# Attention of a hybrid encoder step on one TensorE: both kv heads of a pair in one unit

## The chip, the cores and the metric

One core of one Trainium2 chip. The metric is the device time of one execution of the whole program in microseconds (us); for one core that is its own time. TensorE (PE) multiplies, VectorE (DVE), ScalarE (ACT) and GpSimd (POOL) do the element-wise work, and SyncE's queue issues most transfers.

## The reference, cut to what matters

The step runs two trunk layers over 1024 prompt tokens and 8 x 16 sample tokens, 1024 features wide. Layer 0 mixes with S5 and a gated delta rule, layer 1 with sliding-window attention, and each is followed by a gated feed-forward. The change lies in layer 1's attention: 16 heads of 64 features share 4 kv heads (4 heads each), a prompt chunk of 64 tokens sees the keys of its own and the two chunks before, a sample sees 128 cached keys and its own 16, and each row has a sink beside its scores.

```python
scores = jnp.einsum('bnqkgd,bnskd->bnkgqs', q, kband).astype(jnp.float32) * (SWA_HEAD_DIM ** -0.5)
scores = jnp.where(valid[None, :, None, None, None, :], scores, -1e30)
p = sink_softmax(scores, sinks).astype(vband.dtype)
o = jnp.einsum('bnkgqs,bnskd->bnqkgd', p, vband).reshape(bsz, L, SWA_HEADS * SWA_HEAD_DIM)
return o @ wo, k[:, -KV_WIN:], v[:, -KV_WIN:]
```

## The kernel before, in words

Activations lie with features on partitions and tokens on the free axis. A dense product is three float32r passes over operands split into a rounded part and a remainder: `gemm_block` (lines 301 to 311) issues 24 matmuls of 384 tokens into one PSUM bank, and `project` (lines 1502 to 1554) does the same for the output projection by halves of the features, 12 matmuls a half (lines 1514 to 1516). A plain fp32 product, as attention uses, stands in the trace as two matmuls and two weight loads.

`swa` (from line 1776) makes keys `kT` and values `vT`, then the queries of kv pair 0 (`qgemm(0)`), attends with them (`attend(0, ...)`, line 1940), makes the queries of pair 1, splits pair 0's output into operands (lines 1943 to 1946), attends with pair 1 and calls `project`. A pair is two kv heads; the first has its 64 features on the lower half of the partitions, the second on the upper half. `attend` runs 16 prompt units, one for each chunk of 64 tokens, then 8 sample units.

`prompt_unit` (lines 1852 to 1890) loops over the two heads e. For each: two score products into a `pS` bank (line 1862, 64 rows of the array, up to 192 keys); a softmax over both rows groups (`soft`, lines 1833 to 1850); up to four transposes into a `pT` bank (line 1882); one DVE copy of it into `sT` (lines 1885 and 1887); and one or two output products into the head's half of the partitions of a `pO` bank (line 1889), one for each 128-token tile that the keys touch. A chunk from number 2 on touches two tiles, one with all 128 keys and one with 64. After both heads the bank is evicted: by ACT for pair 0 (line 1940), by ACT and then DVE for pair 1 (lines 1951 and 1952). `sample_unit` (lines 1894 to 1914) has both heads in one bank: for each head a score product with 128 cached keys (line 1899) and one with 16 new keys (line 1900), then one softmax, two transposes, a copy, and for each head an output product with the cached values and one with the new ones (lines 1912 and 1913).

`soft` reduces the maximum on DVE (line 1837), makes the negative, clipped maximum (1838) and the sink's term (1839, 1840), takes the exponential of each row group on ACT with its sum (1842), adds and inverts (1843, 1844), and normalises group 0 on POOL (1850) and group 1 on ACT (1848).

Banks and buffers: two banks each for `pS`, `pT` and `pO` (line 1823), three softmax tiles (line 1824), two `sT`. The order of the instructions on each engine is not the source's: a planner (the tile context of line 1973) lists every instruction of the program with its dependences and its reuse of buffers and, for each engine, takes the earliest traced one of those that its own model of time holds ready. `Sooner` (line 260) moves evictions ahead. So dense products that are traced later, those of `qgemm(1)` and of `project`, stand between the attention's products in PE's queue wherever the planner found none of the attention ready; they are called fill below. Once planned, each engine's order is fixed.

Of the kernel before, what the change touches and what calls it, by code (L numbers as in the profile page):

```python
"""Hybrid S5 / gated-DeltaNet / sliding-window encoder step on one core.

Activations are held as [feature on partitions, token on the free axis]; the 1024 prompt tokens come
first, then the 8 x 16 sample tokens. A dense product is three float32r passes over operands split
exactly into a rounded part and its remainder."""
# [10 lines left out]
F32 = mybir.dt.float32  # L16
# [28 lines left out]
def ksplit(w):  # L45
    """[K, M] -> [M/128, 128 (k in its chunk), K/128 * 128] panels."""
    k, m = w.shape
    return np.ascontiguousarray(w.reshape(k // 128, 128, m // 128, 128).transpose(2, 1, 0, 3).reshape(m // 128, 128, k))


def halves(w):
    """[1024, 1024] -> [K halves, M/256, 128, 2 * 512] panels."""
    return np.ascontiguousarray(ksplit(w).reshape(4, 2, 128, 2, 512).transpose(3, 0, 2, 1, 4).reshape(2, 4, 128, 1024))


def cols(v):
    """[n * 128] -> [128, n]."""
    return np.ascontiguousarray(v.reshape(-1, 128).T)


def head_order():
    """Column order of q: row halves of a 128-tile hold a head of an even and of an odd kv group."""
    o = []
    for pair in range(2):
        for i in range(4):
            for par in range(2):
                h = 4 * (2 * pair + par) + i
                o += list(range(64 * h, 64 * h + 64))
    return np.array(o)


def s5_order():
    """Order of the S5 channels inside each 128: (channel of a group, group)."""
    return np.arange(512).reshape(4, 8, 16).transpose(0, 2, 1).reshape(512)


def layout(a):
    """The kernel's inputs: moved, copied and zero-padded only."""
# [52 lines left out]
def constants():  # L131
    """Depend on shapes alone."""
# [55 lines left out]
class Chunks:  # L188
    """Chunks of features in tiles of two: x[:, chunk, tokens]."""
# [4 lines left out]
    def new(self, i, shape, dt=F32):  # L194
        """A tile in the place of the i-th."""
# [7 lines left out]
def body(tc, nc, I, O):  # L203
# [19 lines left out]
    def mphase(**tags):  # L223
        """Five banks for the parts between the dense products: one ring, or one for each of the named tiles."""
# [25 lines left out]
    def behind(i, *others):  # L250
        """Queue an instruction behind others of its engine."""
# [4 lines left out]
    def log_tables(*others):  # L256
        """One load of the tables that Ln and Exp share, behind other activations."""
        return behind(S.preload_act_table_set("natural_log_exp_and_others"), *others)

    class Sooner:  # L260
        """Instructions inside go before others that are ready, as if traced n instructions earlier."""
# [16 lines left out]
    def parts(raw, pool=None, bufs=2):  # L278
        """Rounded part and remainder of a panel of weights."""
# [11 lines left out]
    def slots(name):  # L291
        """Per token block, the rounded part and the remainder of 4 + 4 chunks of features."""
# [24 lines left out]
    def sums(sq, w, tag=None):  # L317
        """Sum over partitions of sq, on all partitions (a bank)."""
# [11 lines left out]
    def square_in(x, k, b, i, new, parts, keep=None):  # L330
        """Squares of a chunk into partial sums over chunks; the partial sums with the last chunk.

        One running sum by GpSimd (and one by VectorE), and the last chunk's squares on their own."""
# [15 lines left out]
    def rms(r, b, parts, first=0):  # L349
        """1 / sqrt(mean of squares + eps) of a block's tokens, on all partitions, from parts of the sums of squares."""  # L350
# [18 lines left out]
    def norm(w, h, r, new, first, keep=None):  # L369
        """What fills the scales and, where there are, the operands of a norm as chunk k of block b of x, its i-th, is final."""  # L370
# [36 lines left out]
    # up_0 = -(0 + 10 + 3 + 14) - z - 1      up_1 = 15 - y - 2 - 5 + 6 + 7       up_2 = y + 0 + 10 + s  # L407
    # with z = 12 + 15, v = 13 + 16, y = 13 - P17 and s = 2 + 5 + P11, each number the product of that number.
# [31 lines left out]
    def reserve(pool):  # L440
        """Place for split panels at the bottom of a pool."""
# [3 lines left out]
    def ffn(x, pre, l, w, nxt):  # L445
# [3 lines left out]
        # gate and up  # L449
# [37 lines left out]
        # sums of weights, split panels, and what the products make  # L487
# [14 lines left out]
        def weights(raw, ps, place=place):  # L502
            """Rounded parts and remainders of the left operands of up to four products."""
# [22 lines left out]
        def tile_of(f, raw, room, order, panels, early=False):  # L526
            """The products of a tile of f: those without the last block of tokens, then the others."""
# [9 lines left out]
            def prods(p, *ps, more=False):  # L537
                """Products into p; more of them, added to what has been read already."""
# [126 lines left out]
        # the first two tiles of f, while the operands of the twenty are made  # L665
# [48 lines left out]
        # x comes back; until then half of its place is for more panels  # L714
# [19 lines left out]
        # down, by pairs of tiles of f; the products of two pairs go to sums of the seven over all pairs  # L734
# [17 lines left out]
        def load(f):  # L752
            """A tile of f, and room for another block."""
# [12 lines left out]
        def right(ps, last):  # L766
            """Right operands of two pairs, and places for those of the pair that is multiplied plainly."""
# [28 lines left out]
        def into(terms, m, o, first=False):  # L796
            """The products of the terms, tile m of their columns, added to o."""
# [10 lines left out]
        # the last pair is multiplied plainly, and what it gives added with products of the seven that make the same part of x  # L808
        also = {"B21": (0, 1), "T4": (4, 1), "B22": (0, 2)}
        for j in range(0, len(pairs) - 1, 2):  # L810
# [24 lines left out]
            for q in range(4):  # L835
# [5 lines left out]
                for e, n in enumerate(PANELS[q]):  # L841
                    for m in range(4):
# [6 lines left out]
                        if last:  # L849
                            # the sums of the seven make x  # L850
# [26 lines left out]
    # ------------------------------------------------------------------ layer 0  # L877
# [98 lines left out]
    # b and a rows: beta, cumulative log decay and what follows from it  # L976
# [26 lines left out]
    def gate_in(hh, zz):  # L1003
        """The gate of a head."""
# [8 lines left out]
    # S5: u, chunk operators, and the states after each chunk  # L1013
# [11 lines left out]
    # powers 1 to 16 of the step over a chunk  # L1025
# [32 lines left out]
    # prompt: scans inside 8 groups of 16 chunks, then over the groups' ends, then what each group starts with  # L1058
# [27 lines left out]
    # convolutions, and what of the delta rule needs no recurrence  # L1086
# [35 lines left out]
    def l2norms(ys, tables):  # L1122
        """Scale pairs (y, scratch, log of a factor) to unit length of every token."""
# [60 lines left out]
    # inverses of the delta rule's triangular systems' blocks: 32 tokens, one block to a partition  # L1184
# [29 lines left out]
    # S5 outputs  # L1214
# [28 lines left out]
    # v  # L1243
# [25 lines left out]
    # S5: operands of the GLU  # L1269
# [16 lines left out]
    # delta rule, recurrence over 128-token tiles  # L1286
# [13 lines left out]
    def solved(TT, kg, vt, t, uu, wt, tag):  # L1300
        """u and w of a tile from the transposed inverse of its system."""
# [18 lines left out]
    def finish(o, zs, t):  # L1320
        """Gated norm of a tile's output, into the operands of the output projection."""
# [16 lines left out]
    def solve_pair(t):  # L1338
        """Transposed inverses of the systems of tiles t and t + 1."""
# [13 lines left out]
        # the inverse's off-diagonal blocks, from 32 to 64 and from 64 to 128: -T11 B T00  # L1353
# [32 lines left out]
    # delta rule, the samples' step  # L1386
# [91 lines left out]
    # GLU, and the output projection of its half  # L1478
# [25 lines left out]
    def project(name, ap, x, opnd, view, w, between, places=()):  # L1504
        """An output projection, into x and the operands of the next norm: the first half of its features, but most of it for
# [471 lines left out]
```

## Time and profile before

| | |
|---|---|
| Median of 3 runs | 2831.71 us (2828.5 to 2837.01) |
| Span of the profiled execution | 2835.9 us; no other time is given for this execution |
| PE busy | 2618.7 us, 92% of the span |
| DVE, POOL, ACT busy | 1977.8, 1639.5, 1103.2 us |
| First to last score product of the stage | 1616.0 to 1914.2 us |
| Last eviction of the stage | 1934.1 us |

How to read it: busy time of PE counts the matmuls that the trace shows; two that overlap count once. A row of the timeline merges neighbours of one line: its first number is the start in us from the span's start, its second the length from there to the end of the last of them, and the last (x4) how many there are. The granted clock is a share of full speed, 1.00 being 2.4 GHz and 0.50 being 1.2 GHz.

### The profile page before, as it was taken

The numbers are of one execution on the slowest core, as the hardware profiler recorded it, in microseconds if no ns is written. First come the engines' busy times: TensorE is split into PE (matmuls) and PEld (weight loads), VectorE is DVE, ScalarE is ACT, GpSimd is POOL, SyncE is SP. The second block draws the span as 40 slices with busy tenths as digits, with TensorE's granted clock in tenths as the row PEclk, the third lists the DMA queues.
The fourth block names the chain that finished last, engine by engine and source line by source line (L and its number), as shares of the span: only waits on it lengthen the run. The fifth ranks groups of instructions, "written<-read, shape, count | busy, mean of one in ns | idle before, by whom it ended". The sixth has DMA issues, their size and how long they took to land.

```text
span 2835.9 us, 40158 instructions
## 1 busy us (share of the span) xinstructions
PE 2618.7 (92%) x14777; PEld 2422.3 (85%) x14777; DVE 1977.8 (70%) x3195; ACT 1103.2 (39%) x2232; POOL 1639.5 (58%) x1659
## 2 busy tenths in 40 slices
PE   7898999998799999989999999998799999989996
PEld 6787898897799899989999966668789999979996
DVE  7757855568876666698866245557877666688977
ACT  4233574443433333343333144433333333344332
POOL 8659332225687777788532012114587777788744
PEclk9999999998899999989999999898899999989998
DMA  6523376531122222243213100202022222243311
GB/s 199 155 74 98 107 248 205 180 121 66 56 94 70 70 70 70 70 161 120 91 43 108 59 16 23 89 29 97 32 92 78 75 71 71 70 144 106 110 62 67
DMA packets 164165, 267.20 MB, mean 94 GB/s; under 512 B 34189, under 2 KB 123949, under 8 KB 162929
## 3 DMA queue, kind: packets, MB, share of 16 engines
q1 hardware_dynamic: 163392, 262.28, 28.8%
q8 instruction: 116, 1.90, 0.3%
q10 hardware_dynamic: 576, 2.36, 0.2%
q14 instruction: 81, 0.66, 0.1%
HBM read 186.92 MB, written 79.51 MB: 94 GB/s over the span
## 4 chain that ended last, share of the span: by engine, by line
PE 45%; POOL 22%; DVE 17%; DMA 7%; issue 5%; ACT 3%; SPq 1%; DVEq 0%; ACTq 0%; POOLq 0%
POOL x L518 8%; POOL cm L518 5%; PE pd L436 4%; PE pd L437 4%; PE pd L438 4%; DMA raw<-in_wu_dram 3%; PE pg L307 3%; PE pg L308 3%; PE pg L309 3%; DVE wlo L523 3%; PE pO L1889 2%; DMA raw<-in_wg_dram 2%; PE pg L1514 2%; PE pS L1862 2%; PE pg L1516 2%
## 5 line engine op out<-in xcount | busy, mean ns | idle before, releaser
L518 POOL TENSOR_TENSOR x<-raw 128x256 f32<-128x256 f32 (+1 forms) x372 | 353.1, 976 | 99.0 <-DMA raw<-in_wg_dram 85.5
L436 PE MATMUL pa<-u,whi 128*128 128x384 f32 x928 | 324.8, 350 | 41.4 <-DVE bt L555 14.3
L438 PE MATMUL pa<-u,wlo 128*128 128x384 f32 x928 | 311.2, 345 | 13.7 <-DVE wlo L523 13.7
L437 PE MATMUL pa<-u,whi 128*128 128x384 f32 x928 | 319.2, 344 | 1.7 <-DVE u L469 1.5
L518 POOL TENSOR_TENSOR cm<-raw 128x256 f32<-128x256 f32 (+1 forms) x244 | 236.2, 990 | 78.4 <-DVE wlo L523 28.0
L436 PE MATMUL pd<-g,whi 128*128 128x384 f32 x708 | 240.4, 340 | 0.9 <-DVE bt L555 0.9
L437 PE MATMUL pd<-g,whi 128*128 128x384 f32 x708 | 241.1, 341 | 0.0
L438 PE MATMUL pd<-g,wlo 128*128 128x384 f32 x708 | 238.2, 338 | 0.0
L436 PEld LDWEIGHTS pa<-u,whi 128*128 128x128 f32 x928 | 180.7, 195 | 55.6 <-DVE bt L555 15.9
L523 DVE TENSOR_TENSOR wlo<-x,whi 128x1024 fp32r<-128x1024 f32 (+1 forms) x132 | 155.4, 1177 | 101.7 <-ACT whi L522 101.3
L1850 POOL TENSOR_SCALAR p<-p,rd 128x192 f32<-128x192 f32 (+3 forms) x80 | 59.1, 741 | 287.4 <-DVE rd L1844 175.5
L522 ACT CAST whi<-x 128x1024 fp32r<-128x1024 f32 (+1 forms) x132 | 115.7, 876 | 236.8 <-POOL x L518 209.6
L438 PEld LDWEIGHTS pa<-u,wlo 128*128 128x128 f32 x928 | 179.2, 194 | 17.3 <-DVE wlo L523 17.3
L284 ACT CAST whi<-raw 128x1024 fp32r<-128x1024 f32 x113 | 116.3, 1049 | 178.1 <-PE pg L308 83.0
L437 PEld LDWEIGHTS pa<-u,whi 128*128 128x128 f32 x928 | 180.5, 195 | 3.4 <-DVE u L469 2.3
L436 PE MATMUL pa<-u,x 128*128 128x384 f32 x428 | 150.6, 352 | 31.0 <-ACT x L522 26.8
L285 DVE TENSOR_TENSOR wlo<-raw,whi 128x1024 fp32r<-128x1024 f32 x113 | 162.4, 1438 | 22.3 <-ACT whi L284 22.1
L437 PE MATMUL pa<-u,x 128*128 128x384 f32 x428 | 148.9, 348 | 0.0
L307 PE MATMUL pg<-h0h,whi 128*128 128x384 f32 x384 | 136.6, 356 | 12.4 <-DVE ut L941 11.4
L438 PE MATMUL pa<-u,x 128*128 128x384 f32 x428 | 143.9, 345 | 0.0
L764 DVE TENSOR_TENSOR g<-gf,g 128x384 fp32r<-128x384 f32 x132 | 136.7, 1062 | 5.8 <-ACT g L763 5.8
L436 PEld LDWEIGHTS pd<-g,whi 128*128 128x128 f32 x708 | 133.9, 189 | 1.7 <-DVE bt L555 1.6
(727 smaller groups left out, 7946.2 us busy)
## 6 DMA issues: line engine op xcount, KB each, us to landing
gf<-d_g SPq DMA_DIRECT2D x44, 576.0 KB
raw<-in_wg_dram SPq DMA_DIRECT2D x44, 512.0 KB
raw<-in_wu_dram SPq DMA_DIRECT2D x44, 512.0 KB
raw<-in_wd_dram SPq DMA_DIRECT2D x44, 512.0 KB
raw<-in_win_dram SPq DMA_DIRECT2D x21, 512.0 KB
d_r<-x SPq DMA_DIRECT2D x24, 384.0 KB
x<-d_r SPq DMA_DIRECT2D x8, 1152.0 KB
d_aq<-AQ SPq DMA_DIRECT2D x12, 576.0 KB
```

Source lines behind the costliest of these rows:

```text
L284: S.copy(hi, raw)
L285: V.tensor_sub(lo, raw, hi)
L307: PE.matmul(p[:, :BW], hi[:, c], rh, start=(i == 0), stop=False)
L308: PE.matmul(p[:, :BW], hi[:, c], rl, start=False, stop=False)
L309: PE.matmul(p[:, :BW], lo[:, c], rh, start=False, stop=(i == len(ks) - 1))
L436: PE.matmul(p, hi[:, c], uh, start=start, stop=False, skip_group_check=more)
L437: PE.matmul(p, hi[:, c], ul, start=False, stop=False, skip_group_check=more)
L438: PE.matmul(p, lo[:, c], uh, start=False, stop=stop, skip_group_check=more)
L518: (P.tensor_add if sg > 0 else P.tensor_sub)(cm[:, 256 * j:256 * (j + n)], fa, ga)
L522: S.copy(hi[:, c], src)
L523: V.tensor_sub(lo[:, c], src, hi[:, c])
L764: eng.tensor_sub(op[1], t, op[0])
```

## The change

A prompt unit takes both heads together. All four score products are issued at the unit's start, alternating between the heads (row halves) and into a bank for each head. One softmax covers four row groups, with the per-unit scalars four wide. The transposes and the copy follow head by head, and then the output products, tile by tile and alternating between the heads (column halves of one bank). A sample unit has one score product of 144 keys for each head, since the 16 new keys are copied by POOL behind the 128 cached ones, and its output products alternate as well. `pS` has four banks, `pT` and `pO` one each; the softmax tiles are two of twice the rows; `sT` has three buffers; the offset of the scores in a softmax tile changes with the parity of the chunk.

```diff
-    env["mphase"](pS=2, pT=2, pO=2)
-    NPT = 3
-    pt_ = [wk.tile([128, 2, 320], F32, name=f"p{i}") for i in range(NPT)]
+    env["mphase"](pS=4, pT=1, pO=1)
+    NPT = 2
+    pt_ = [wk.tile([128, 4, 256], F32, name=f"p{i}") for i in range(NPT)]
...
-    def soft(pS, pt, n, na, sink, off):
+    def soft(banks, pt, n, sink, off):
         sink, minus = sink
+        na = sink.shape[-1]
         ng, su, es, rd = (small(x) for x in ("ng", "su", "es", "rd"))
-        V.tensor_reduce(ng[:, :na], pS, mybir.AxisListType.X, ALU.max)
+        g = na // len(banks)
+        for i, pS in enumerate(banks):
+            V.tensor_reduce(ng[:, g * i:g * i + g], pS, mybir.AxisListType.X, ALU.max)
...
-            S.activation(pt[:, a, off:off + n], pS[:, a, :], AF.Exp, scale=0.125, bias=ng[:, a:a + 1], accum_out=su[:, a:a + 1])
+            S.activation(pt[:, a, off:off + n], banks[a // g][:, a % g, :], AF.Exp, scale=0.125, bias=ng[:, a:a + 1], accum_out=su[:, a:a + 1])
...
-            if a:
+            if a % 2:
...
     def prompt_unit(pair, c, out):
+        k0 = max(0, 64 * (c - 2))
+        n = 64 * (c + 1) - k0
+        pSv = [mbank("pS")[:, :2 * n].rearrange("p (a k) -> p a k", a=2) for e in range(2)]
+        for a in range(2):
+            for e, hs in enumerate(halves_):
+                PE.matmul(pSv[e][:, a], qpr[pair][hs, c, 2 * a:2 * a + 2, :].rearrange("p i k -> p (i k)"), kT[hs, pair, k0:k0 + n], start=True, stop=True)
+        pt = next_pt()
+        off = k0 - 64 * (c - 2) + (64 if c % 2 else 0)
+        soft(pSv, pt, n, [t[:, 4 * pair:4 * pair + 4] for t in (snk[:, 0], snk[:, 1])], off)
...
         for e in range(2):
             pT = mbank("pT")
...
+            V.tensor_copy(sT[:, :nk].rearrange("p i a k -> p (i a k)"), pT[:, :256 * nk])
+            sTs.append(sT)
+        pO = mbank("pO")
+        for i, (t, w, lo, hi) in enumerate(ks):
+            for e, hs in enumerate(halves_):
+                kv = 2 * pair + e
+                PE.matmul(pO[hs, :256], vT[lo:hi, t, 64 * kv:64 * kv + 64], sTs[e][lo:hi, i].rearrange("p a k -> p (a k)"), start=(i == 0), stop=(i == nk - 1))
         out(c, pO[:, :256].rearrange("p (i k) -> p i k", i=4))
...
     def sample_unit(pair, b, out, ck, cvt, vn):
         pS = mbank("pS")
-        for e in range(2):
-            hs = slice(64 * e, 64 * e + 64)
-            ql = qsa[pair][hs, b].rearrange("p i k -> p (i k)")
-            PE.matmul(pS[hs, 0:128], ql, ck[hs, b, :], start=True, stop=True)
-            PE.matmul(pS[hs, 128:144], ql, kT[hs, pair, TP + LS * b:TP + LS * b + LS], start=True, stop=True)
+        for hs in halves_:
+            PE.matmul(pS[hs, 0:144], qsa[pair][hs, b].rearrange("p i k -> p (i k)"), ck[hs, b, :], start=True, stop=True)
...
-        for e in range(2):
-            hs = slice(64 * e, 64 * e + 64)
+        for hs in halves_:
             PE.matmul(pO[hs, :64], cvt[:, b, hs], sT[:, 0, 0, hs], start=True, stop=False)
+        for hs in halves_:
             PE.matmul(pO[hs, :64], vn[:, b, hs], sT[0:16, 0, 1, hs], start=False, stop=True)
...
-        ck = wk.tile([128, NS, 128], F32, name="ck", tag="ck", bufs=1)
-        Q.dma_start(ck, I["ck"][:, pair].rearrange("b p t -> p b t"))
+        ck = wk.tile([128, NS, 144], F32, name="ck", tag="ck", bufs=1)
+        Q.dma_start(ck[:, :, 0:128], I["ck"][:, pair].rearrange("b p t -> p b t"))
+        P.tensor_copy(ck[:, :, 128:144], kT[:, pair, TP:].rearrange("p (b t) -> p b t", b=NS))
```

## Rows read from the trace of the kernel before

**Rows 1.** The page: PE's busy time, and the chain that ended last, by engine.
```profile
PE 2618.7 (92%) x14777; PEld 2422.3 (85%) x14777; DVE 1977.8 (70%) x3195; ACT 1103.2 (39%) x2232; POOL 1639.5 (58%) x1659
...
PE 45%; POOL 22%; DVE 17%; DMA 7%; issue 5%; ACT 3%; SPq 1%; DVEq 0%; ACTq 0%; POOLq 0%
```
**Rows 2.** Busy time by stretch: length, engines, granted clock, DMA share, GB/s.
```profile
1616.00:1936.00 320.00, 319.30 (x1638) 223.53 (x1638) 168.28 (x565) 131.89 (x505) 65.97 (x86) 0.93 0.13 42
...
1761.00:1795.00 34.00, 33.70 (x123) 22.47 (x122) 16.25 (x65) 14.06 (x63) 6.66 (x11) 0.50 0.48 173
```
**Rows 3.** Waits, 1616 to 1936 us: waiter, releaser, us, times, longest.
```profile
PE pO L1889 <- DVE sT L1887: 0.3, 1, 0.3
...
DVE sT L1885 <- PE pT L1882: 36.0, 34, 3.0
```
**Rows 4.** The chain of waits from 1616 to 1936 us, by line.
```profile
by line: PE pO L1889 22.0%; PE pS L1862 18.0%; PE pT L1882 10.2%; PE pg L1514 7.4%; PE pg L1516 6.6%; PE pg L1515 6.3%; PE pg L308 6.2%; PE pg L309 5.9%; PE pg L307 5.9%; PE pO L1912 3.3%; PE pO L1913 3.3%; PE pT L1907 2.0%; PE pS L1899 2.0
```
**Rows 5.** The timeline: one head's transposes, their copy, the output product after it.
```profile
1661.60 0.60 PE L1882 MATMUL pT<-ident,p 128*128 128x128 f32 x4
...
1662.23 0.69 DVE L1885 COPY sT<-pT 128x512 f32<-128x512 f32 x1 [2.00 <-PE pT L1882]
...
1667.74 1.22 PE L1889 MATMUL pO<-sT,vT 64*64 64x256 f32 x4
```
**Rows 6.** The timeline, PE: scores of one head, and of two next to each other.
```profile
1627.32 0.92 PE L1862 MATMUL pS<-kT,q 64*128 64x192 f32 x4
...
1655.90 0.91 PE L1862 MATMUL pS<-kT,q 64*128 64x192 f32 x4
...
1742.80 0.93 PE L1862 MATMUL pS<-kT,q 64*128 64x192 f32 x8
...
1800.70 0.93 PE L1862 MATMUL pS<-kT,q 64*128 64x192 f32 x8
```
**Rows 7.** The timeline, PE: scores at the lower clock.
```profile
1784.04 1.65 PE L1862 MATMUL pS<-kT,q 64*128 64x192 f32 x4
...
1790.94 1.65 PE L1862 MATMUL pS<-kT,q 64*128 64x192 f32 x4
```
**Rows 8.** The timeline, ACT: the two exponentials of one head.
```profile
1650.10 0.42 ACT L1842 ACTIVATE p<-pS,ng 128x192 f32<-128x192 f32 x1 [1.61 <-DVE ng L1838]
...
1650.51 0.41 ACT L1842 ACTIVATE p<-pS,ng 128x192 f32<-128x192 f32 x1
```
**Rows 9.** The timeline, PE: output products of one head, and of two in succession.
```profile
1659.81 1.22 PE L1889 MATMUL pO<-sT,vT 128*64 128x256 f32 x4
...
1797.38 2.37 PE L1889 MATMUL pO<-sT,vT 128*64 128x256 f32 x8
```
**Rows 10.** The timeline, PE: an S5 product by column halves, and transposes.
```profile
142.85 1.25 PE L1049 MATMUL pe<-U,LB 128*64 128x144 f32 x16
...
1751.09 1.09 PE L1882 MATMUL pT<-ident,p 128*128 128x128 f32 x8
```
**Rows 11.** The timeline, PE: the four transposes of one head, issued apart.
```profile
1856.98 0.27 PE L1882 MATMUL pT<-ident,p 128*128 128x128 f32 x1
...
1858.33 0.55 PE L1882 MATMUL pT<-ident,p 128*128 128x128 f32 x3
```
**Rows 12.** The timeline, PE: sample units (scores of one head, of two; output products).
```profile
1757.36 0.43 PE L1899 MATMUL pS<-ck,q 64*64 64x128 f32 x2
...
1758.16 0.44 PE L1899 MATMUL pS<-ck,q 64*64 64x128 f32 x4
...
1758.61 0.33 PE L1912 MATMUL pO<-sT,cvt 128*64 128x64 f32 x2
...
1759.63 0.44 PE L1907 MATMUL pT<-ident,p 128*128 128x128 f32 x2
```
**Rows 13.** Groups by line, 1616 to 1936 us: busy, mean ns, idle before them.
```profile
L1850 POOL TENSOR_SCALAR p<-p,rd 128x192 f32<-128x192 f32 (+3 forms) x80 | 59.1, 741 | 287.4 <-DVE rd L1844 175.5 <-DVE es L1839 48.2 <-DVE ng L1838 19.4
...
L1952 DVE TENSOR_TENSOR o1l<-pO,o1h 128x256 fp32r<-128x256 f32 (+1 forms) x24 | 8.5, 353 | 14.9 <-ACT o1h L1951 14.9
```

More of the change, by code (lines that the diff above doesn't have):

```diff
@@ L1828, in swa, with small @@
     npt = [0]
-    def small(n, w=2):
+    def small(n, w=4):
         return wk.tile([128, w], F32, name=n, tag=n, bufs=4)
-    def soft(pS, pt, n, na, sink, off):
+    def soft(banks, pt, n, sink, off):
         sink, minus = sink
+        na = sink.shape[-1]
         ng, su, es, rd = (small(x) for x in ("ng", "su", "es", "rd"))
-        V.tensor_reduce(ng[:, :na], pS, mybir.AxisListType.X, ALU.max)
+        g = na // len(banks)
+        for i, pS in enumerate(banks):
+            V.tensor_reduce(ng[:, g * i:g * i + g], pS, mybir.AxisListType.X, ALU.max)
         V.scalar_tensor_tensor(ng[:, :na], ng[:, :na], -0.125, minus, ALU.mult, ALU.min)
@@ L1850, in soft, with next_pt @@
                 P.tensor_scalar(q, q, rd[:, a:a + 1], None, op0=ALU.mult)
+    halves_ = [slice(0, 64), slice(64, 128)]
+    def next_pt():
+        npt[0] += 1
+        return pt_[npt[0] % NPT]
     def prompt_unit(pair, c, out):
-        pO = mbank("pO")
-        for e in range(2):
-            hs = slice(64 * e, 64 * e + 64)
-            kv = 2 * pair + e
-            k0 = max(0, 64 * (c - 2))
-            n = 64 * (c + 1) - k0
-            pS = mbank("pS")
-            pSv = pS[:, :2 * n].rearrange("p (a k) -> p a k", a=2)
-            for a in range(2):
-                PE.matmul(pSv[:, a], qpr[pair][hs, c, 2 * a:2 * a + 2, :].rearrange("p i k -> p (i k)"), kT[hs, pair, k0:k0 + n], start=True, stop=True)
-            pt = pt_[npt[0] % NPT]
-            npt[0] += 1
-            off = k0 - 64 * (c - 2) + 64
-            soft(pSv, pt, n, 2, [t[:, 2 * kv:2 * kv + 2] for t in (snk[:, 0], snk[:, 1])], off)
-            t1 = c // 2
-            ks = []
-            w0 = 64 if c % 2 == 0 else 0
-            for t, w in ((t1 - 1, w0), (t1, w0 + 128)):
-                if t < 0:
-                    continue
-                lo = max(k0, 128 * t) - 128 * t
-                hi = min(64 * (c + 1), 128 * t + 128) - 128 * t
-                if hi > lo:
-                    ks.append((t, w, lo, hi))
@@ L1878, in prompt_unit @@
+        t1 = c // 2
+        ks = []
+        for t, w in ((t1 - 1, 0), (t1, 128)):
+            if t < 0:
+                continue
+            lo = max(k0, 128 * t) - 128 * t
+            hi = min(64 * (c + 1), 128 * t + 128) - 128 * t
+            if hi > lo:
+                ks.append((t, w, lo, hi))
+        nk = len(ks)
+        sTs = []
+        for e in range(2):
             pT = mbank("pT")
-            sT = wk.tile([128, 2, 2, 128], F32, name="sT", tag="sT", bufs=2)
+            sT = wk.tile([128, 2, 2, 128], F32, name="sT", tag="sT", bufs=3)
@@ L1880, in prompt_unit @@
             for i, (t, w, lo, hi) in enumerate(ks):
                 for a in range(2):
-                    PE.transpose(pT[:, (2 * i + a) * 128:(2 * i + a) * 128 + 128], pt[:, a, w:w + 128], ident)
-            nk = len(ks)
-            if nk == 2:
-                V.tensor_copy(sT.rearrange("p i a k -> p (i a k)"), pT)
-            else:
-                V.tensor_copy(sT[:, 0].rearrange("p a k -> p (a k)"), pT[:, :256])
-            for i, (t, w, lo, hi) in enumerate(ks):
-                PE.matmul(pO[hs, :256], vT[lo:hi, t, 64 * kv:64 * kv + 64], sT[lo:hi, i].rearrange("p a k -> p (a k)"), start=(i == 0), stop=(i == nk - 1))
+                    PE.transpose(pT[:, (2 * i + a) * 128:(2 * i + a) * 128 + 128], pt[:, 2 * e + a, w:w + 128], ident)
@@ L1890, in prompt_unit @@
+            V.tensor_copy(sT[:, :nk].rearrange("p i a k -> p (i a k)"), pT[:, :256 * nk])
[5 more added lines that the diff above has]
+                PE.matmul(pO[hs, :256], vT[lo:hi, t, 64 * kv:64 * kv + 64], sTs[e][lo:hi, i].rearrange("p a k -> p (a k)"), start=(i == 0), stop=(i == nk - 1))
         out(c, pO[:, :256].rearrange("p (i k) -> p i k", i=4))
-    ns = npt
@@ L1894, in sample_unit @@
     def sample_unit(pair, b, out, ck, cvt, vn):
         pS = mbank("pS")
-        for e in range(2):
-            hs = slice(64 * e, 64 * e + 64)
-            ql = qsa[pair][hs, b].rearrange("p i k -> p (i k)")
-            PE.matmul(pS[hs, 0:128], ql, ck[hs, b, :], start=True, stop=True)
-            PE.matmul(pS[hs, 128:144], ql, kT[hs, pair, TP + LS * b:TP + LS * b + LS], start=True, stop=True)
-        pt = pt_[npt[0] % NPT]
-        npt[0] += 1
-        soft(pS[:, :144][:, None, :], pt, 144, 1, [t[:, pair:pair + 1] for t in (snks[:, 0], snks[:, 1])], 64)
+        for hs in halves_:
+            PE.matmul(pS[hs, 0:144], qsa[pair][hs, b].rearrange("p i k -> p (i k)"), ck[hs, b, :], start=True, stop=True)
@@ L1904, in sample_unit @@
+        pt = next_pt()
+        soft([pS[:, :144][:, None, :]], pt, 144, [t[:, pair:pair + 1] for t in (snks[:, 0], snks[:, 1])], 0)
         pT = mbank("pT")
-        sT = wk.tile([128, 2, 2, 128], F32, name="sT", tag="sT", bufs=2)
+        sT = wk.tile([128, 2, 2, 128], F32, name="sT", tag="sT", bufs=3)
         for i in range(2):
-            PE.transpose(pT[:, i * 128:i * 128 + 128], pt[:, 0, 64 + 128 * i:192 + 128 * i], ident)
+            PE.transpose(pT[:, i * 128:i * 128 + 128], pt[:, 0, 128 * i:128 + 128 * i], ident)
@@ L1908, in sample_unit @@
         V.tensor_copy(sT[:, 0].rearrange("p a k -> p (a k)"), pT[:, :256])
         pO = mbank("pO")
-        for e in range(2):
-            hs = slice(64 * e, 64 * e + 64)
+        for hs in halves_:
             PE.matmul(pO[hs, :64], cvt[:, b, hs], sT[:, 0, 0, hs], start=True, stop=False)
+        for hs in halves_:
             PE.matmul(pO[hs, :64], vn[:, b, hs], sT[0:16, 0, 1, hs], start=False, stop=True)
```

## The prediction

> **What bounds the kernel now.** The page comes first: TensorE (PE) is busy for 92% of the span, and PE work is 45% of the chain that ended last [rows 1]. Then the stage: the changed code runs from 1616 us, the first score product, to 1936 us, the last evictions. The stretch table [rows 2] shows PE busy for 319.3 of these 320 us, VectorE (DVE) for 168, ScalarE (ACT) for 132, GpSimd (POOL) for 66. The waits agree: PE itself is held up twice, for 0.3 us each, while DVE spends 36.0 us waiting for transposes alone [rows 3]. So PE's own issue time sets this stage, and the chain by line [rows 4] divides it: 22.0% (70 us) for the prompt's output products, 18.0% (58 us) for its scores, 10.2% (33 us) for its transposes, 3.3% twice for the samples' output products (21 us). The rest is mostly dense products that the planner puts between, the "fill".
>
> Two further readings decide how a faster PE would be used. First the lag: transposes at 1661.60 are copied at 1662.23, and the output product that reads this copy starts at 1667.74 [rows 5]. (Copies and products run in one order, and two older copies still have their products ahead.) Some 4.8 us lie between the end of the copy and its reader, filled with PE work that was ahead in the order. Where there is fill, every product is thus late by PE's backlog, not by its input. Second the stretch from 1761 to 1795, whose table row shows a granted clock of 0.50, against 0.93 over the whole stage [rows 2]: no fill runs there, and four score matmuls take 1.65 us there against 0.91 [rows 6, 7].
>
> **The change part by part.** The traced execution has a span of 2835.9 us, and no other time of it is given; the median of the runs is 2831.7, so the trace lies 4.2 us above it, inside their spread. I take the sum off the span and carry the same difference to the median.
>
> *Scores.* One head's two products are four matmuls in the trace (an fp32 product runs as two passes): 0.91 us. Where the planner happened to put both heads next to each other, eight take 0.93 us [rows 6]: heads on different row halves run beside each other. The gain is 0.85 to 0.9 us a unit. There are 32 units (16 chunks, two pairs); four have short key ranges and two of the others are paired already, so at most 26 x 0.88 = 23 us. It asks that both heads stand together in PE's order. The two banks of an older unit come free after its second and its fourth exponential, two steps of 0.41 us apart [rows 8], so the planner can issue head 0 first and put fill between. Bounds 0 and 23; I take two thirds, **-15 us**, since the two release times lie closer together than one head's products take.
>
> *Output products.* Now a head's four matmuls (two tiles of keys) take 1.22 us, and two heads in succession 2.37 [rows 9], though they go to different column halves. Each head's two products use different row counts (128 and 64), and in this order nothing overlaps. The new order is tile 0 of both heads, then tile 1 of both. That column halves can run beside each other shows in the S5 stage: 16 matmuls of 144 columns, 128 rows and 64 columns of the array take 1.25 us, where eight of 128 columns on the whole array take 1.09 [rows 10]; in succession the 16 would need over 2.1. But the first product of head 0 needs only head 0's copy, and head 1's copy comes at least one transpose-and-copy later, since one pT bank is left. In the rows of 1857 a single transpose is issued and the three others of its bank 1.4 us later, one of which needed nothing more than the first: I read that as program order kept inside a bank [rows 11]. So head 0's first product goes alone, then head 1's first, then the last two as a pair: two passes' time saved per unit. A pass costs 70 us / 240 = 0.29, so 0.59 x 28 units with two tiles = **-16 us**. Bounds: 0 (nothing together) and -33 (both tiles paired).
>
> *Samples.* Four output products take 1.02 us (1758.61 to 1759.63) [rows 12] and all wait for the same copy, so cvt pairs with cvt, vn with vn: half, 16 units x 0.51 = 8 us. Scores lose the separate 16-column products: the heads already overlap (four matmuls in 0.44, two in 0.43), and the eight last 0.45 us (1758.16 to 1758.61) against some 0.3 for four of 144 columns: 16 x 0.15 = 2. Together **-10 us**, bounds -3 and -12.
>
> *Fewer banks.* pT and pO fall from two banks to one, pS rises from two to four. With fill, head 1's transposes waiting for head 0's copy (0.69 us and 0.04 of start) cost PE nothing: the 4.8 us backlog covers it. Without fill they cost about 0.75 us a unit. Some twelve units would run without fill: the 34 us of [rows 2], at 6.9 us a unit [rows 7], are five units' worth, and I expect more at the end of either pair, since a unit now waits more and so takes more fill. That is **+9 us**; bounds 0, and 32 x 0.75 = +24. With one pO bank a unit's first output product waits for the previous eviction; units are 8.9 us apart now (chunk 2 at 1627.32, chunk 15 at 1742.80) [rows 6], and the DVE subtraction that ends an eviction takes 0.35 to 0.42 us [rows 13], so 0.
>
> *Half clock.* The 34 us at 0.50 are some 15 us dearer than the same work elsewhere (34 x (1 - 0.91/1.65)) [rows 6, 7]. I leave that as it is, 0; bounds -15 (gone) and +15 (twice as long).
>
> *The rest costs nothing while PE binds.* The per-unit scalars (four DVE operations and an exponential) are made once instead of twice; two POOL copies for the ck tile and larger memsets are added, and POOL idles 287 us before its 80 normalisations [rows 13], which cover them. If PE stopped binding, the scalars saved would be a gain, and POOL's copies would come on top of its normalisations. POOL's copy for pair 1 has to wait until pair 0's last sample is scored; behind it stand pair 1's normalisations, which need later products anyway. The three loads per pair stay, one of them into rows of 144 instead of 128 words.
>
> Sum: -15 - 16 - 10 + 9 = -32 us: 2804 on the trace's basis, **2800 us** as a median.
>
> **A rule against it.** The rows give overlap for two products on one half followed by two on the other: line 1047 loops over the halves outside and over the products of a half inside, in one bank, yet the 16 matmuls take 1.25 us [rows 10]. The Trainium skill, TensorE: Matmul & The Clock Gate, Part 3, says that matmuls start and end strictly in program order. By that rule a two-pass product could share only its second pass with the next product's first; the trace disagrees, since those products would then hardly share anything. What that ordering would make of this kernel is rival C.
>
> **Rivals.**
> A, full pairing: the order on the chip is the order of the source, all scores and both tiles paired. -23 - 33 - 10 + 9 = -57: 2775. For it: the rows of overlap; against it: one pT bank, which parts the two copies. Chance 0.14.
> B, pairs in name only: the planner parts the heads of both kinds, and only the samples gain: -10 + 9, and I add nothing: 2831. For it: in the kernel before, products of both halves met only twice among the long units [rows 6]. Against it: two score banks per unit are now allocated together. Chance 0.12.
> C, passes in order: four passes of a pair share one slot instead of two, so pairs of products give half, alternating scores three slots of eight instead of four. -11 - 8 - 5 + 9 = -15: 2817. The rows speak against it. Chance 0.07.
> D, slower: the fill runs out. With one pT bank a unit passes two lags in turn, 2 x (4.8 + 0.6 + 0.7) = 12 us [rows 5] against 8.9 now, so it takes more fill; fill is fixed, ends several units early in each pair, and what is left runs at half clock. There a unit takes 6.9 us (chunk 3 at 1784.04, chunk 4 at 1790.94) [rows 7] where scores of 0.93, three outputs of 0.59 and eight transposes of 0.136 make 3.7, so each costs 3.2. Ten such units take the gain of 32 away, and from 13 on the kernel is slower by over 8.5 us; 14 give +13: 2845. For it: the clock row. Against it: fill for pair 1 also comes from the second half of the projection. Chance 0.07.
> My forecast, between them: 0.60.
>
> **How the numbers follow.** A measurement of this kernel tells 0.3% (8.5 us) from no change. Faster: forecast, A and C, 0.60 + 0.14 + 0.07 = 0.81; same: B, 0.12; slower: D, 0.07. Range: the forecast's own terms reach from -15 (scores 0, rest as taken) to -48 (output fully paired); taking in A's centre and the upper wait gives 2772 to 2826. That leaves out D, most of B and A's lower tail, about 2 in 10.
>
> **What would show it.** Right: L1862's successor rows show eight matmuls in some 0.95 us in most units; output rows show two matmuls alone, then six in about 1.8 us; chain shares of pO and pS in the stage fall to some 50 and 40 us; the last eviction of the stage comes some 30 us sooner, and later stages keep their length. Wrong: score rows of four 0.9 us long with fill between (then B); eight output matmuls in 1.2 us (then A); PE waits of many us on DVE copies, or a granted clock of 0.50 over far more than 34 us (then D).

## The result, and the profile after

The changed kernel takes **2851.65 us** (median of 4 runs, 2849.28 to 2855.65) against 2830.11 us for the kernel before on the same chip: ratio 1.0074, 95% interval 1.0062 to 1.0086. It is slower, by 0.7%, and the prediction (2772 to 2826 us) was wrong. The profiled execution took 2849.57 us and has a span of 2847.8 us.

The page's PE line and chain by engine answer to [rows 1]. PE was busy for 9 us less in a span 12 us longer: the loss is time in which PE waited, or work done at the lower clock.

```profile
PE 2609.9 (92%) x14713; PEld 2413.3 (85%) x14713; DVE 1972.1 (69%) x3067; ACT 1101.0 (39%) x2200; POOL 1637.6 (58%) x1660
...
PE 46%; POOL 20%; DVE 17%; DMA 7%; issue 5%; ACT 3%; SPq 1%; DVEq 0%; ACTq 0%; POOLq 0%
```

The stretch table answers to [rows 2], with its columns. In the same 320 us PE is now busy for 298.4 and not 319.3, at a mean clock of 0.83 and not 0.93. With two levels, 1.00 and 0.50, a mean of 0.83 is 34% of the time at the lower one, 109 us, against 45 us before. The stage itself now ends at 1954 us, not at 1934. The loss does not lie in the first part (1646 to 1697: never idle, full clock), but after it.

```profile
1616.00:1936.00 320.00, 298.40 (x1440) 205.01 (x1440) 153.06 (x403) 121.01 (x436) 56.89 (x79) 0.83 0.11 37
1646.00:1697.00 51.00, 51.00 (x276) 40.49 (x275) 21.13 (x46) 17.54 (x56) 7.52 (x10) 1.00 0.07 22
...
1713.00:1743.00 30.00, 27.43 (x84) 14.45 (x83) 12.57 (x31) 12.32 (x43) 5.76 (x8) 0.50 0.00 1
```

The waits of the same 320 us answer to [rows 3]. PE was held up for 0.6 us in all before; now it waits for exponentials 28 times. ACT's exponentials in turn wait 58.7 us for transposes: a head's rows of a softmax tile come free when the transposes of that head two units earlier have read them.

```profile
ACT p L1846 <- PE pT L1890: 58.7, 55, 4.8
DVE sT L1891 <- PE pT L1890: 50.1, 37, 4.9
...
PE pS L1869 <- ACT p L1846: 10.3, 15, 1.0
PE pS L1903 <- ACT p L1846: 8.3, 13, 1.2
```

The chain by line answers to [rows 4]: outputs fell from 22.0 to 18.5%, scores and transposes rose, and ACT's exponentials, with no share among the lines shown before, now hold 6.0%.

```profile
by line: PE pS L1869 19.6%; PE pO L1897 18.5%; PE pT L1890 11.9%; PE pg L1514 6.3%; ACT p L1846 6.0%; PE pg L1515 5.8%; PE pg L1516 5.6%; PE pg L308 5.1%; PE pg L307 5.1%; PE pg L309 5.0%; PE pS L1903 2.3%; PE pT L1909 1.5%; DVE sT L1891 1.
```

Two stretches of the timeline say why. Where there is fill (left out here: all the time between these rows is PE's, on dense products), one unit reads:

```profile
1661.65 0.66 PE L1890 MATMUL pT<-ident,p 128*128 128x128 f32 x4
...
1662.29 0.42 ACT L1846 ACTIVATE p<-pS,ng 128x192 f32<-128x192 f32 x1 [0.16 <-PE pT L1890]
1662.34 0.69 DVE L1891 COPY sT<-pT 128x512 f32<-128x512 f32 x1 [2.40 <-PE pT L1890]
...
1666.66 0.60 PE L1890 MATMUL pT<-ident,p 128*128 128x128 f32 x4
...
1667.18 0.65 PE L1897 MATMUL pO<-sT,vT 128*64 128x256 f32 x2
1667.24 0.42 ACT L1846 ACTIVATE p<-pS,ng 128x192 f32<-128x192 f32 x1 [2.87 <-PE pT L1890]
1667.29 0.69 DVE L1891 COPY sT<-pT 128x512 f32<-128x512 f32 x1 [0.40 <-PE pT L1890]
...
1671.76 1.23 PE L1897 MATMUL pO<-sT,vT 128*64 128x256 f32 x6
...
1672.91 0.66 PE L1890 MATMUL pT<-ident,p 128*128 128x128 f32 x4
```

Head 0's transposes at 1661.65, their copy, head 1's transposes 5.0 us after head 0's, their copy, and the next unit's 6.3 us later: one bank, two turns, 11.3 us a unit against 8.9 before. The copy that frees the bank is over at 1663.03; what keeps head 1's transposes back for 3.6 us more are the dense products that the planned order puts ahead of them. The output products stand as forecast, two alone (0.65) and then six in 1.23 us. The exponentials of the two heads start 5 us apart, each behind its transposes, and so the two score banks come free 5 us apart too: groups of four score matmuls of 0.91 us, as before.

The dense products of pair 1's queries end at 1697 (1740 before); only 24 of the projection's can stand between until 1800. Of the first pair, units 8 to 15 run there. On PE alone:

```profile
1704.19 0.66 PE L1890 MATMUL pT<-ident,p 128*128 128x128 f32 x4
1705.80 0.91 PE L1869 MATMUL pS<-kT,q 64*128 64x192 f32 x4 [0.95 <-ACT p L1846]
1706.65 0.66 PE L1890 MATMUL pT<-ident,p 128*128 128x128 f32 x4
1707.23 0.65 PE L1897 MATMUL pO<-sT,vT 128*64 128x256 f32 x2
1708.26 0.92 PE L1869 MATMUL pS<-kT,q 64*128 64x192 f32 x4 [0.38 <-ACT p L1846]
1709.10 1.23 PE L1897 MATMUL pO<-sT,vT 128*64 128x256 f32 x6
1710.26 0.65 PE L1890 MATMUL pT<-ident,p 128*128 128x128 f32 x4
...
1718.25 1.12 PE L1890 MATMUL pT<-ident,p 128*128 128x128 f32 x4
...
1727.55 1.11 PE L1890 MATMUL pT<-ident,p 128*128 128x128 f32 x4
```

A unit takes 6.1 us at the upper clock, 1.33 of it PE's waits (0.95 + 0.38), and 9.3 us (1718.25 to 1727.55) once the clock has fallen.

The samples' eight output matmuls now take 0.53 us at the upper clock (1927.05 to 1927.58, the transposes behind them), where [rows 12] had 1.02 us.

```profile
1927.05 0.34 PE L1913 MATMUL pO<-sT,cvt 128*64 128x64 f32 x4
1927.32 0.33 PE L1915 MATMUL pO<-sT,vn 16*64 16x64 f32 x4
1927.58 0.44 PE L1909 MATMUL pT<-ident,p 128*128 128x128 f32 x2
```

### The profile page after: what moved, and what is told of

Read it like the earlier page. It is cut to its first block, busy times and chain, and to the rows that moved or that the text cites. A ratio compares the mean times of both kernels' runs of the same rounds, so it can differ in the third digit from the quotient of the medians.

```text
span 2847.8 us, 39745 instructions
## 1 busy us (share of the span) xinstructions
PE 2609.9 (92%) x14713; PEld 2413.3 (85%) x14713; DVE 1972.1 (69%) x3067; ACT 1101.0 (39%) x2200; POOL 1637.6 (58%) x1660
## 4 chain that ended last, share of the span: by engine, by line
PE 46%; POOL 20%; DVE 17%; DMA 7%; issue 5%; ACT 3%; SPq 1%; DVEq 0%; ACTq 0%; POOLq 0%
POOL x L518 8%; PE pd L436 4%; PE pd L437 4%; PE pd L438 4%; POOL cm L518 4%; DVE wlo L523 3%; PE pg L307 3%; PE pg L309 3%; PE pg L308 3%; DMA raw<-in_wg_dram 3%; PE pS L1869 2%; PE pO L1897 2%; DMA raw<-in_wu_dram 2%; PE pg L1514 2%; PE b L438 2%
```

## The experiments

The name of a kernel gives its banks in the order pS, pT, pO. Ratios are to the kernel before on the same chip, with their 95% intervals; a difference between two kernels of this section is uncertain by some 7 to 8 us either way, an estimate from the intervals of the two ratios (more for the kernels whose interval is wider).

**Which bank?** Two kernels change the banks of the changed kernel, two those of the kernel before.

```diff
-    env["mphase"](pS=4, pT=1, pO=1)
+    env["mphase"](pS=3, pT=2, pO=1)
```

> The changed kernel with pS=3, pT=2, pO=1 in place of 4, 1, 1. Theory P (the one transpose bank): where there is fill, a unit passes transposes, copy, transposes, copy in turn through one bank, each turn late by PE's backlog of 4 to 5 us, so 11.3 us a unit where the kernel before takes 8.9; fill is then gone 43 us too early. With two banks both heads' transposes stand at once: a unit takes 8.9 us or less, fill reaches 1735 us or later, and the time is 2800 to 2825. Rival Q (the one output bank, which also passes two turns a unit): stays at 2845 to 2860. Rival R (one softmax for both heads over two tiles, whatever the banks): stays at 2843 to 2860.

Measured: 2785.52 us, ratio 0.9843 (0.9828 to 0.9859), 66 us below the changed kernel. The direction is P's, but the time lies 14.5 us under P's range (2800 to 2825).

```diff
-    env["mphase"](pS=4, pT=1, pO=1)
+    env["mphase"](pS=3, pT=1, pO=2)
```

> The changed kernel with pS=3, pT=1, pO=2: the control with the same score banks, the freed bank given to the output. Theory P: units stay at 11.3 us and the time at 2845 to 2860. Rival Q: units under 9 us and 2800 to 2825. Rival R: 2843 to 2860.

Measured: 2857.99 us, 1.0097 (1.0073 to 1.0122). Q and R fall: neither a second output bank nor the shared softmax makes the difference. The timeline of the 3, 2, 1 kernel shows both heads' transposes next to each other, and units 4 and 14 of the first pair at 1648.52 and 1725.91: ten units in 77.4 us, 7.7 us each. That is less than the 8.9 us that P allowed, so the dense products of pair 1's queries are used up by 1725.4 us and not at 1735 or later, as P had it.

```profile
1648.52 0.60 PE L1890 MATMUL pT<-ident,p 128*128 128x128 f32 x4
1649.14 0.60 PE L1890 MATMUL pT<-ident,p 128*128 128x128 f32 x4
...
1662.12 0.64 PE L1897 MATMUL pO<-sT,vT 64*64 64x256 f32 x2
1663.40 1.22 PE L1897 MATMUL pO<-sT,vT 64*64 64x256 f32 x6
...
1725.91 0.44 PE L1890 MATMUL pT<-ident,p 128*128 128x128 f32 x2
```

Its stretch table for the stage: PE waits 1.3 us in 282, and the clock is 0.95 (28 us at the lower level).

```profile
1616.00:1898.00 282.00, 280.67 (x1576) 200.99 (x1576) 151.60 (x427) 123.29 (x462) 66.40 (x88) 0.95 0.14 48
```

Next the kernel before, with the bank alone and with all the banks of the change.

```diff
-    env["mphase"](pS=2, pT=2, pO=2)
+    env["mphase"](pS=2, pT=1, pO=2)
```

> The kernel before with pS=2, pT=1, pO=2 in place of 2, 2, 2: one bank for the transposes and nothing else of the change. Theory P: units of 11.3 us as in the changed kernel, without its shorter outputs and samples, so 15 to 30 us slower than the changed kernel's loss: 2855 to 2885. Rivals Q and R: within 8 us of the kernel before, 2822 to 2838.

```diff
-    env["mphase"](pS=2, pT=2, pO=2)
+    env["mphase"](pS=4, pT=1, pO=1)
```

> The kernel before with the banks of the change, pS=4, pT=1, pO=1, and nothing else. Theory P: as with the one transpose bank alone, 2855 to 2885, within 8 us of it. Rival Q: slower as well, 2850 to 2880, but the kernel with one transpose bank alone is not. Rival R: 2822 to 2838.

Measured: 2886.38 us, 1.0210 (1.0158 to 1.0263), and 2863.72 us, 1.0119 (1.0091 to 1.0146). One transpose bank costs the old code 55 us, a microsecond more than P's range held; its timeline has the transposes of one head and the next mostly 6.25 us apart (below), 12.5 us a unit. With 4, 1, 1 it loses 32, 23 less than with one bank alone and not within the 8 us that P said: the other banks of that division give something back, which no run here takes apart.

```profile
1665.93 0.66 PE L1882 MATMUL pT<-ident,p 128*128 128x128 f32 x4
1672.18 0.66 PE L1882 MATMUL pT<-ident,p 128*128 128x128 f32 x4
```

**What is each gain worth once the bank is mended?** Two kernels undo one alternation each, on 3, 2, 1 banks.

```diff
-        for i, (t, w, lo, hi) in enumerate(ks):
-            for e, hs in enumerate(halves_):
+        for e, hs in enumerate(halves_):
+            for i, (t, w, lo, hi) in enumerate(ks):
```

> The changed kernel with 3, 2, 1 banks, its output products head by head again (both tiles of head 0, then both of head 1). If the alternation of output products is what shortens them, the six-matmul groups of 1.2 us go, eight take 2.3 to 2.4 us in place of 1.75, and with PE the bound again that is 0.59 us for each of 28 units: 2798 to 2808. Rival (PE no longer binds, so shorter products are only refilled with waiting): within 6 us of the same kernel with alternating products, 2780 to 2791.

Measured: 2808.05 us, 0.9927 (0.9906 to 0.9948). Alternating the output products is worth 22.5 us, at the top of what was expected; the eight stand in succession again:

```profile
1650.63 2.37 PE L1897 MATMUL pO<-sT,vT 128*64 128x256 f32 x8
```

```diff
         for hs in halves_:
             PE.matmul(pO[hs, :64], cvt[:, b, hs], sT[:, 0, 0, hs], start=True, stop=False)
-        for hs in halves_:
             PE.matmul(pO[hs, :64], vn[:, b, hs], sT[0:16, 0, 1, hs], start=False, stop=True)
```

> The changed kernel with 3, 2, 1 banks, the samples' output products head by head again, their single score product kept. If the pairing of these is worth what the rows say (1.02 us halved in 16 units), 5 to 12 us slower than with them alternating: 2790 to 2798. Rival (samples run where PE waits anyway): within 4 us, 2781 to 2790.

Measured: 2797.49 us, 0.9887 (0.9869 to 0.9905): 12.0 us.

**Why did no scores pair?** The exponentials are taken alternately from the two score banks.

```diff
-        for a in range(na):
+        for a in sorted(range(na), key=lambda a: a % 2):
```

> The changed kernel with 3, 2, 1 banks, its four exponentials taken alternately from the two score banks (head 0, head 1, head 0, head 1), so that these come free one exponential apart and not two. Theory Z (the release times keep the heads' score products apart): groups of eight score matmuls of 0.93 us in most units, 0.85 us saved in each: 2762 to 2778. Rival Y (the ring of three banks, or the planner, parts the heads anyway): groups of four as before and 2778 to 2792.

Measured: 2769.60 us, 0.9778 (0.9754 to 0.9803), 15.9 us under the same banks without it, and the fastest kernel of this study. Its timeline has 21 groups of eight score matmuls (5 without the edit); one of them, and eight output matmuls that all pair:

```profile
1649.76 0.93 PE L1869 MATMUL pS<-kT,q 64*128 64x192 f32 x8
...
1658.42 1.23 PE L1897 MATMUL pO<-sT,vT 128*64 128x256 f32 x8
```

So the order of the exponentials decides whether scores pair. That it does so by release times on the chip, as theory Z has it, is not shown: in the kernel without the edit the exponentials of one unit are over at 1671.14, some 3 us before the next unit's score products start (1674.33 and 1675.72), and two dense products stand between these. What parts the heads there is the planned order, fixed beforehand.

The same edit with the banks of the change, 4, 1, 1:

> The changed kernel with its own banks, 4, 1, 1, and alternating exponentials alone. If the release times keep the heads' score products apart and nothing else, groups of eight score matmuls appear and the time falls to 2825 to 2842. If the one transpose bank also parts them (the exponentials of head 0 and of head 1 wait for their softmax rows, freed by transposes 5 us apart): an alternate order makes all wait for the later one, units get no shorter, and the time is 2843 to 2865.

Measured: 2842.79 us, 1.0033 (1.0013 to 1.0054), between the two ranges. The timeline decides: groups of four, four groups of eight in the stage (three in the changed kernel), transposes of head 0 still 11.3 us apart (below). So with one transpose bank the order of the exponentials does not bring the heads together. Its 9 us are little more than the noise of such a difference, and no run takes them apart.

```profile
1649.33 0.66 PE L1890 MATMUL pT<-ident,p 128*128 128x128 f32 x4
...
1655.48 0.91 PE L1869 MATMUL pS<-kT,q 64*128 64x192 f32 x4
...
1660.65 0.66 PE L1890 MATMUL pT<-ident,p 128*128 128x128 f32 x4
```

Two other divisions of the six banks, both with alternating exponentials; in the second, outputs take their turn in the transpose banks.

```diff
-    env["mphase"](pS=4, pT=1, pO=1)
+    env["mphase"](pS=2, pT=2, pO=2)
```

> The same alternating exponentials with 2, 2, 2 banks: the two score banks are always the two heads of one unit. Theory Z: groups of eight score matmuls in nearly all units; what that saves (up to 24 us) is partly given back since only one unit's scores can be in flight: 2765 to 2800. Rival Y: groups of four, and 2785 or more.

```diff
-    env["mphase"](pS=4, pT=1, pO=1)
+    env["mphase"](pS=4, pT=2, pO="pT")
```

> The changed kernel with alternating exponentials, four score banks and two banks that transposes and outputs share in turn. If scores gain most from banks that always belong in pairs, and the shared ring (three uses of two banks a unit, each of some 5.5 us) stays under the unit's 7 us: 2755 to 2770. If the shared ring binds (8 to 9 us a unit, fill gone early): 2785 to 2815.

Measured: 2786.17 us, 0.9839 (0.9824 to 0.9853), with 14 groups of eight and 31 of four, so its time fits both readings and tells nothing between them; and 2803.11 us, 0.9891 (0.9875 to 0.9908), in the range for a shared ring that binds: a unit takes 10.4 us there (head 0's transposes at 1644.26, 1654.66 and 1665.07), more than the 8 to 9 expected.

**Is it the missing fill?** The queries of pair 1 are made ahead of pair 0's attention, with the changed banks and with 3, 2, 1.

```diff
     qgemm(0)
+    qgemm(1)
     attend(0, lambda c, k, src: S.copy(o0[:, c, :, k], src))
-    qgemm(1)
```

> The changed kernel with the queries of pair 1 made ahead of pair 0's attention, so that pair 0 has no fill. Theory P1 (the one transpose bank is dear only where dense products stand between a copy and its reader; a turn is then some 1.5 us and not 5): a two-tile unit of pair 0 takes 8.5 to 10 us at the lower clock, or 5.5 to 6.5 us at the upper, and at most 1.5 us longer than in the same kernel with 3, 2, 1 banks. Rival P2 (the one bank itself costs a unit the 3.8 us that it costs among fill): 3 us or more longer. The whole time: slower than with fill, 2880 to 2960, since nothing stands beside pair 0.

> The same with 3, 2, 1 banks. P1: a two-tile unit of pair 0 is 0 to 1.5 us shorter than with 4, 1, 1 banks; P2: 3 us or more shorter. The whole time by P1: pair 0 gains up to 24 us and pair 1, which has fill from the projection, 20 to 35 us: 2830 to 2920.

Measured, in two runs each: 2880.31 us, 1.0163 (1.0143 to 1.0184), and 2786.62 us, 0.9833 (0.9810 to 0.9855). P1 fell on its own number, P2's (3 us or more) holds, and the expectation for 3, 2, 1 was 43 us too high: with two transpose banks the attention of pair 0 can do with hardly any fill. Quite without it neither is: two groups of 12 dense products of the projection stand in pair 0's stretch, at 1720.61 and 1775.44 with one bank, at 1694.01 and 1721.12 with two. The stretch tables and timelines of pair 0, first with one bank:

```profile
1667.00:1725.00 58.00, 53.97 (x156) 30.27 (x155) 23.33 (x62) 23.91 (x88) 11.73 (x16) 0.50 0.00 1
```

```profile
1697.97 1.12 PE L1890 MATMUL pT<-ident,p 128*128 128x128 f32 x4
1699.93 1.65 PE L1869 MATMUL pS<-kT,q 64*128 64x192 f32 x4 [0.85 <-ACT p L1846]
...
1707.27 1.11 PE L1890 MATMUL pT<-ident,p 128*128 128x128 f32 x4
```

and with two:

```profile
1664.00:1674.00 10.00, 10.00 (x35) 5.75 (x35) 4.80 (x16) 5.24 (x24) 2.68 (x4) 0.51 0.00 0
...
1680.00:1727.00 47.00, 45.52 (x275) 28.43 (x273) 32.25 (x89) 32.94 (x134) 19.02 (x22) 1.00 0.01 1
```

```profile
1685.88 0.66 PE L1890 MATMUL pT<-ident,p 128*128 128x128 f32 x4
1686.51 0.91 PE L1869 MATMUL pS<-kT,q 64*128 64x192 f32 x4
1687.35 0.66 PE L1890 MATMUL pT<-ident,p 128*128 128x128 f32 x4
1687.94 0.91 PE L1869 MATMUL pS<-kT,q 64*128 64x192 f32 x4
1688.78 1.24 PE L1897 MATMUL pO<-sT,vT 64*64 64x256 f32 x8
1689.95 0.65 PE L1890 MATMUL pT<-ident,p 128*128 128x128 f32 x4
```

The units shown take 9.30 us with one bank and 4.07 with two. In the first, PE waits in each unit (0.85 in the rows) and the clock is 0.50; in the second it hardly waits (1.5 of the 47 us) and the clock is 1.00. At the upper clock the changed kernel's unfed unit took 6.07 us, so about 2.0 of the 5.2 us are the bank's waits and the products that do not pair, and the other 3.2 the clock. Why the clock stays low with one bank is not shown by this: with two banks it was low as well from 1664 to 1674 us, with PE busy all the time, and rose in the midst of the attention.

## Why the prediction was wrong, step by step

**Fewer banks, +9 (bounds 0 and 24): the step that failed.** It said that with fill, head 1's transposes waiting for head 0's copy "cost PE nothing: the 4.8 us backlog covers it", and priced some twelve unfed units at 0.75 us each. The first half is true of PE's busy time and misses the point: the backlog does not hide a turn of the bank, it lengthens it. A unit passes two turns, 5.0 and 6.3 us, and so lasts 11.3 us (without fill, at the upper clock, the turns are 2.5 and 3.6 us: 1704.19, 1706.65, 1710.26). Fill was gone for 15 units, 8 of the first pair and 7 of the second, and such a unit costs 2.0 us more than with two banks at the upper clock and 5.2 with the clock that goes with it, not 0.75. Measured, the division 4, 1, 1 costs 66 us against 3, 2, 1 (2851.65 - 2785.52), nearly three times the upper bound; since 3, 1, 2 gains nothing, that is the transpose bank's. By the stretch tables some 20 us of it are PE's waits (21.6 against 1.3). The lower clock has 109 - 28 = 81 us more, 36 us by the prediction's ratio of 0.91 to 1.65. Both together make 56 of the 66, and the stage to its last eviction is 56 us longer (1616 to 1954 us, 338 us, against 282; its last 18 us are busy throughout, at the upper clock). The other 10 lie behind the stage (893.8 us against 884.0), and no run here takes them apart. Whether another order of the same instructions would carry one bank better was not tried.

**Half clock, 0 (bounds -15 and +15).** Wrong with it: 64 us more of it in the same 320 us (109 against 45), some 29 us by that ratio, twice the bound.

**Scores, -15.** Nothing came: three groups of eight in the whole stage. The reason given was that release times 0.82 us apart (two exponentials) are close enough. With one transpose bank the exponentials of the two heads stand 5 us apart; with two they follow each other as reckoned, and still only 5 groups of eight formed. It took the alternate order as well, which the change does not have, and then the gain was 15.9 us, uncertain by some 8: that it meets the 15 so closely is luck.

**Output products, -16.** Right in order and cause: two alone, then six (head 1's copy is late): two passes of 0.29 and, from the start of the six at 1709.10 to the transposes at 1710.26, 1.16, together 1.74 us where 2.37 - 0.59 = 1.78 was reckoned. The sentence on what would show it gave the six 1.8 us by themselves, a slip. Undone on the mended kernel it was worth 22.5 us, under the bound of 33; there, where both copies are done in time, all eight pair (in 1.23 us at 1708.31), as rival A had it. Why two heads in succession overlap nowhere (2.37 us), while the S5 products, one half after the other in the source, do [rows 10], no run takes apart.

**Samples, -10.** Right within the noise: 12.0 us for the output products alone, 8 forecast. The single score product was not undone by itself.

**The sum without the failed term** was -41, and the mended kernel is 46.3 us faster than before (2831.80 to 2785.52). That the two are so close is partly luck: scores gave none of their 15, outputs and samples 34.5 in place of 26, and 17 us less at the lower clock (28 against 45) some 8 that were not in the sum. Of the 54 us between the two profiled executions, 38 lie in the stage (320 against 282) and 16 behind it (899.9 against 884.0), which no run here takes apart.

**Slips in the working** that do not change the outcome: with scores at 0 and with outputs fully paired the forecast's terms sum to -17 and -49, not -15 and -48; from -17 the upper wait leads to 2830, not 2826; D's unit sums to 3.8, not 3.7; and when the copy of 1662.23 was made, one older copy and not two still had its product ahead, at 1663.70.

**The rivals.** D had the mechanism, two turns of one bank (12 us forecast, 11.3 measured), 2845 us with 14 unfed units (15 ran so); the prediction gave it 0.07 although it worked out the 12 us from its own rows and knew that fill is fixed. Its reason was half right: running out of fill need cost nothing, as the kernel with two banks and 24 dense products in pair 0's stretch shows. What costs is that with one bank PE then waits and the clock is low. B was right that the heads' scores stay apart, and wrong on the outputs. C fell: the eight output matmuls at 1688.78 end their issue at 1689.95, 1.17 us later, four passes of 0.29. The Trainium skill, TensorE: Matmul & The Clock Gate, Part 3, would have matmuls start and end in program order. If each pass counts as a matmul, two passes of a head followed by two of the other make five slots, 1.45 us, and the trace disagrees: the first two passes alone, one of each head, take 0.44 us together, where one takes 0.43. If a product of two passes counts as one, these rows keep to that order.

## What to carry to other kernels

Count how often a unit passes through its scarcest buffer in turn, and multiply by the time from a producer to its next use as the trace has it, queue backlog included: if that exceeds the present time of a unit, the buffer binds, even where other work hides the waits. Before banks are moved from one ring to another, time that ring alone in the old code; here one line showed 55 us. Products of two heads overlap only if they stand next to each other in the planned order: here the order of the exponentials, far from the products, decided that (21 groups of eight against 5).

## What was not expected of the hardware

Attention with little between its products (24 dense products in two groups) ran at the upper clock for 47 us (PE busy 45.52), where much the same products with short waits in each unit ran at the lower one for 58 us (53.97 busy). Busy time alone does not tell the two apart: the kernel before had 33.70 of 34.00 us busy at 0.50 [rows 2], and the kernel with two banks itself ran its attention from 1664 to 1674 us at 0.51, busy all the time. Its clock had fallen after waits of 2.10 and 0.62 us (up to 1663.44) and rose at 1674, with no dense product since 1658. With one bank the clock rose to 1.00 within the 12 dense products at 1720.61 and had fallen again by 1733, after waits of 0.95 and 0.38 us. What it takes to raise the clock is left open by these rows. The Trainium skill, TensorE: Matmul & The Clock Gate, Part 1, section "A second HAM failure mode: psum-queue depth-cycling", tells of a kernel whose clock swung because PE idled briefly between groups as it cycled through PSUM banks. The one-bank kernels agree with that (0.50 at waits of 0.85 us a unit), the row of the kernel before does not show such waits.
